# Last down products over 512 and 256 columns, squares of the last norm summed on VectorE, final scaling in two-row steps

## Chip, core and metric

One core of a Trainium2 chip runs the whole program. The metric is the device time of one execution in microseconds. The engines are TensorE (PE: matrix products, with PEld for the loading of weights), VectorE (DVE), ScalarE (ACT), GpSimd (POOL), and SyncE (SP), which here only issues DMAs.

## What is computed

A decoder layer for 2048 prompt tokens and 64 sample tokens of width 1024: a mixer (windowed attention and pooling), cross-attention into 256 memory tokens, a squared-ReLU MLP with 4096 hidden units, and a last RMS norm. Only the end matters here:

```python
h = _rmsnorm(x, g_ffn)
x = x + jnp.square(jax.nn.relu(h @ w_up)) @ w_down
...
y = _rmsnorm(x, g_final)     # x * rsqrt(mean(x*x) + 1e-5) * g_final
```

The inputs and outputs are float32. Each product is made of three products of rounded parts (`fp32r`): weight high by data high, weight high by data low, weight low by data high (`mm3`, lines 109 to 114).

## The kernel before

**Tiling.** Activations lie transposed: 128 of the 1024 features of a row of `x` on the partitions, tokens along the free axis. A token block has eight such rows, `bl.x(0)` to `bl.x(7)`, one behind the other in one tile, each `bl.n` columns wide. The tokens are worked through in three superblocks of two blocks (`SBLOCKS`, line 24): 384 and 384 columns, 256 and 320 (64 of them sample tokens), 384 and 384. In each superblock the whole layer runs, and at its end the MLP: 16 chunks of hidden units, each with an `up` (line 1283) and, for one chunk or for two at a time, a `down` (line 1331). `up` writes the squared-ReLU activations as high and low parts, 384 columns for each of the two halves of the columns, into `H`; in the first and last superblock half 0 is block 0 and half 1 is block 1 (`halves`, line 1175).

**The last down.** `down([NP - 2, NP - 1], ..., True, ...)` (line 1407) is the last one of a superblock, called with `fin`. It goes through half 0 first and then half 1 (`seq`, line 1333), eight rows `m` in each. For each row TensorE makes 12 products (four blocks of hidden units by three parts) into one PSUM bank `ps` out of four (`MM`); VectorE adds the bank onto `x` (line 1350, called the evacuation here); then `norm.sq(m)` takes the row's squares for the last norm.

**The last norm.** `Norm.sq` (line 234) has two ways. By default ScalarE squares the row (line 246 for the first, 249 for the others) and VectorE adds the squares up into `acc` (line 250); `fin` then sums `acc` over the partitions with one float32 product with a matrix of 1/1024 (line 258), which appears in the trace as two instructions. With `on_pe`, which is set for block 1 of the last superblock alone (line 1337), ScalarE squares each row (line 239) and TensorE adds it up in PSUM with a product of its own (line 242), eight pairs of instructions in all. `fin` ends with Ln and Exp on ScalarE (lines 261, 262) and three dependent steps on VectorE (lines 263 to 265), which give the factor `r` for each token.

**The final scaling.** `final(bl)` (line 1367) calls `fin`, multiplies the eight rows by `r` and the gain on VectorE (line 1371), and after each second row issues a store of two rows to `y` on SP (line 1373). It is put on a list `later` with a count (`DEFF`, line 370: 2), which `flush()` lowers; in the last down `flush` is called after the second and the fourth row of each four (line 1354). A `yield` in `final` would let the rest wait for the next `flush`; it is taken in the middle superblock only (`has`, line 1374). What is left on the list at the end is run by `flush(True)` (line 1416).

**Order.** The program is written in this order, but a planner puts each engine's instructions in their order before the kernel runs, and may pass one that is not ready. Within an engine the order then is fixed.

Of the kernel before, what the change touches and what calls it, by code (L numbers as in the profile page):

```python
# [11 lines left out]
AF = mybir.ActivationFunctionType  # L12
ALU = mybir.AluOpType

P = 128
NB = 384
SEQ = 2048
# [12 lines left out]
V_GMIX, V_GMEM, V_GCROSS, V_GFFN, V_GFINAL = 0, 8, 16, 24, 32  # L30
# [21 lines left out]
def kernel(ctx: ExitStack, tc: tile.TileContext, io, nW=12, nF=6, nT=10):  # L52
    nc = tc.nc
# [10 lines left out]
    TS = Slots([sb(f"t{i}", 400) for i in range(nT)])  # L64
    XT = [sb("x0", 3136), sb("x1", 3136)]
    MM = Slots([psp.tile([P, 512], F32, name=f"mm{i}", tag=f"mm{i}") for i in range(4)])
    AUX = Slots([psp.tile([P, 512], F32, name=f"aux{i}", tag=f"aux{i}") for i in range(4)])
# [6 lines left out]
    ones = sb("ones", P)  # L74
# [3 lines left out]
    vec = sb("vec", V_N)  # L78
# [27 lines left out]
    def w8(t):  # L106
        return t[:].rearrange("p (k c) -> p k c", c=P)

    def mm3(ps, ks, Wh, Wl, Hh, Hl, first=True, final=True):
        last = len(ks) - 1  # L110
        for i, k in enumerate(ks):
            nc.tensor.matmul(ps, Wh(k), Hh(k), start=first and i == 0, stop=False)  # L112
            nc.tensor.matmul(ps, Wh(k), Hl(k), start=False, stop=False)  # L113
            nc.tensor.matmul(ps, Wl(k), Hh(k), start=False, stop=final and i == last)  # L114
# [54 lines left out]
    NP = 16  # L169
# [38 lines left out]
    for s in range(3):  # L208
# [12 lines left out]
        for p in range(NP):  # L221
            add_up(s, p)
            pl = (p - 1, p) if p == NP - 1 or s == 1 and p % 2 else () if p == NP - 2 or s == 1 else (p,)
# [4 lines left out]
    class Norm:  # L228
        def __init__(self, n, x, on_pe=False, add=None):
            self.n, self.x, self.on_pe, self.add = n, x, on_pe, add or nc.vector  # L230
            self.acc = None
            self.pm = AUX.get() if on_pe else None

        def sq(self, k, eng=None):
            n = self.n
            if self.on_pe:
                t = TS.get()
                if eng is None:
                    nc.scalar.activation(t[:, 0:n], self.x(k), AF.Square)
                else:  # L240
                    eng.tensor_tensor(t[:, 0:n], self.x(k), self.x(k), ALU.mult)
                nc.tensor.matmul(self.pm[:, 0:n], ones[:], t[:, 0:n], start=k == 0, stop=k == 7)
                TS.put(t)
            elif self.acc is None:
                self.acc = TS.get()
                nc.scalar.activation(self.acc[:, 0:n], self.x(k), AF.Square)
            else:
                t = TS.get()
                nc.scalar.activation(t[:, 0:n], self.x(k), AF.Square)
                self.add.tensor_tensor(self.acc[:, 0:n], self.acc[:, 0:n], t[:, 0:n], ALU.add)  # L250
                TS.put(t)

        def fin(self):
            n = self.n
# [113 lines left out]
    later = []  # L368
    RW = 5
    DEF, DEFF = (1, 1), (2, 2)  # L370
# [188 lines left out]
    def superblock(s, blks, nxt):  # L559
        last, has = s == 2, s == 1  # L560
# [352 lines left out]
        while len(qdone) < len(lead):  # L913
            m = len(qdone)
# [257 lines left out]
        if has:  # L1172
            halves = [[(blks[0], 0, 0, 256), (blks[1], 288, 256, 32)], [(blks[1], 0, 0, 288)]]
        else:
            halves = [[(bl, 0, 0, bl.n)] for bl in blks]
        hn = halves[1][0][3]
        PT = 288 if has else NB
# [3 lines left out]
        tt = {}  # L1181
# [92 lines left out]
        def relu2(H, h, k, t):  # L1274
            for bl, c0, o, w in halves[h]:
                nc.vector.scalar_tensor_tensor(t[:, o:o + w], t[:, o:o + w], 0.0, bl.r3[:, c0:c0 + w], ALU.max, ALU.mult)
            nc.scalar.activation(t[:, 0:hn], t[:, 0:hn], AF.Square)
            hi, lo = H[4 * h + 2 * k], H[4 * h + 2 * k + 1]
            nc.scalar.copy(hi, t[:, 0:hn])  # L1279
            nc.vector.tensor_tensor(lo, t[:, 0:hn], f32(hi), ALU.subtract)  # L1280
            TS.put(t)

        def up(p, H=None):

            def prod(w, o, nm):
                ps = AUX.get()
                wk = [(lambda x: lambda i: x[0][:, x[1] + P * i:x[1] + P * i + P])(x) for x in zip(w, o)]
                mm3(ps[:, 0:hn], range(4), *wk, T(nm, 0), T(nm, 1))
                return ps

            def add(t, ps, r, free=True):
                nc.vector.tensor_tensor(t[:, 0:hn], ps[:, 0:hn], r[:, 0:hn], ALU.add)  # L1292
                if free:
                    AUX.put(ps)
                return t

            wa = S.next(("up", s, p, 0))
            p1 = prod(wa, (0, 0), "B11")
            r1 = TS.get()
            nc.scalar.copy(r1[:, 0:hn], p1[:, 0:hn])  # L1300
            AUX.put(p1)
            if H is None:
                H = own([tt.pop(("B11", 0)), tt.pop(("B11", 1))])
            if p == 0:
                flush()
            wb = S.next(("up", s, p, 1))
            p5 = prod(wb, (0, 0), "T1")
            flush()
            p6 = prod(wb, (512, 512), "T2")
            WS.put(*wb)  # L1310
            r2 = add(TS.get(), p6, r1)
            r4 = add(TS.get(), p5, r2, False)
            w22, *wd = S.next(("up", s, p, 2))
            add(r4, prod(wd, (512, 512), "B22"), r4)
            relu2(H, 1, 0, r4)
            flush()
            p7 = prod(wd, (0, 0), "T3")
            WS.put(*wd)
            add(r2, p7, r2)
            relu2(H, 1, 1, add(TS.get(), p5, r2))  # L1320
            p2 = prod(wa, (512, 512), "B21")
            WS.put(*wa)
            relu2(H, 0, 0, add(r1, p2, r1))
            flush()
            p4 = prod((w22, w22), (0, 512), "T4")
            WS.put(w22)
            relu2(H, 0, 1, add(r2, p4, r2))
            S.pump()
            return H

        def down(pl, Hs, fin=False, hook=None):
            K = range(2 * len(pl))
            seq = [(t, h) for h in (0, 1) for t in (0, 1)] if fin else [(t, h) for t in (0, 1) for h in (1, 0)]
            loaded, left, steps = {}, {}, 0
            if fin:
                for bl in blks:
                    bl.norm = Norm(bl.n, bl.x, on_pe=last and bl.b == 1)
            for t, h in seq:
                if t not in loaded:
                    loaded[t] = [S.next(("dn", s, p, t)) for p in pl]  # L1340
                    left[t] = 2
                w = loaded[t]
                for m4 in range(4):
                    m = 4 * t + m4
                    ps = MM.get()
                    mm3(ps[:, 0:hn], K, lambda k: w8(w[k // 2][0])[:, 2 * m4 + k % 2, :], lambda k: w8(w[k // 2][1])[:, 2 * m4 + k % 2, :],
                        lambda k: Hs[k // 2][4 * h + 2 * (k % 2)], lambda k: Hs[k // 2][4 * h + 2 * (k % 2) + 1])
                    for bl, c0, o, n in halves[h]:
                        x = bl.x(m, c0, c0 + n)
                        nc.vector.tensor_tensor(x, ps[:, o:o + n], x, ALU.add)  # L1350
                    if fin:
                        blks[h].norm.sq(m)
                    MM.put(ps)
                    if m4 == 3 or fin and m4 == 1:
                        steps += 1
                        if hook is not None:
                            hook(steps)
                        flush()
                left[t] -= 1
                if left[t] == 0:  # L1360
                    for x in w:
                        WS.put(*x)
                S.pump()
                if fin and t == 1:
                    later.append([DEFF[h], lambda h=h: final(blks[h])])

        def final(bl):
            bl.norm.fin()
            n = bl.n
            for k in range(8):  # L1370
                nc.vector.scalar_tensor_tensor(bl.x(k), bl.x(k), vec[:, V_GFINAL + k:V_GFINAL + k + 1], bl.norm.r[:, 0:n], ALU.mult, ALU.mult)  # L1371
                if k % 2 == 1:
                    nc.sync.dma_start(io["y"][:, bl.xo + (k - 1) * n:bl.xo + (k + 1) * n], XT[bl.b][:, (k - 1) * n:(k + 1) * n])
                    if has and k < 7:
                        yield
            TS.put(bl.norm.r)

        S.resF = 0
        Ht = [ACTS.get(), ACTS.get()]
        H = own(Ht)  # L1380
# [14 lines left out]
            rest0 = norm1_sums(nxt[0])  # L1395
        Hl = list(tt.values())
        H2 = up(NP - 1)
        for bl in blks:
            TS.put(bl.r3)
        ACTS.put(*tt.values())  # L1400
        Hl = [t for t in Hl if id(t) not in {id(x) for x in tt.values()}]
        hook = None
        if nxt is not None:
            S.resW = 4
            later.append([1, rest0])
            hook = lambda i: norm1(nxt[1], 1) if i == 5 else None
        down([NP - 2, NP - 1], [H, H2], True, hook)
        ACTS.put(*Ht, *Hl)

    TS2 = [sb(f"cp{i}", 512) for i in range(2)]  # L1410
# [139 lines left out]
```

## Time and profile before

| | |
|---|---|
| time, median of 3 runs | 2540.4 us (2538.5 to 2542.72) |
| the profiled execution's own time | 2537.34 us |
| its span, first to last instruction | 2535.3 us |
| TensorE busy in the span | 2483.3 us, 98% |
| VectorE busy | 1858.8 us, 73% |
| ScalarE busy | 1098.6 us, 43% |
| GpSimd busy | 172.5 us, 7% |
| granted TensorE clock, mean | 0.992 |

In the profile a line such as `L1371 DVE SCALAR_TENSOR_TENSOR x<-x,vec,t 128x384 f32` names the kernel's line, the engine, the operation, what is written from what, and the shape; buffer numbers are left out, so `x` is any part of the two `x` tiles and `t` any of ten scratch tiles. A busy TensorE is not one at its peak: its products are pipelined, so that one of 0.33 us starts each 0.17 us.

### The profile page before, as it was taken

What the parts mean: (1) busy time and instruction counts of PE and PEld (TensorE: products, weight loads), DVE (VectorE), ACT (ScalarE), POOL (GpSimd) and SP (SyncE); (2) the same over time, 40 slices, a digit from 0 to 9 for tenths busy, and PEclk for the clock granted to TensorE, in tenths of its full rate; (3) what the DMA queues carried; (4) which work ended last, traced back from release to release, by engine and by line L of the source; (5) the groups of instructions that cost most, each with busy time, mean ns of one, the idle gap of its engine ahead of it and who ended that gap; (6) DMA issues with size and microseconds to landing.
All of it is one profiled execution on the core that took longest, in us unless ns stands there. A gap on an engine that the chain in (4) does not pass through costs nothing.

```text
span 2535.3 us, 38897 instructions
## 1 busy us (share of the span) xinstructions
PE 2483.3 (98%) x15199; PEld 2368.2 (93%) x15199; DVE 1858.8 (73%) x3687; ACT 1098.6 (43%) x2131; POOL 172.5 (7%) x282
## 2 busy tenths in 40 slices
PE   9899999999999999999999999999999999999998
PEld 9798989999999998996899999989998999999997
DVE  8568537877777788863787877898745877777775
ACT  7666334433333344752544334457534433333332
POOL 0015010000000001411000000003301000000000
PEclk9999999999999999999999999999999999999999
DMA  8833211222222125246522222240412121222211
GB/s 289 270 122 104 92 34 59 67 67 67 67 67 67 61 81 154 82 148 237 212 92 100 76 92 92 88 143 26 142 42 68 42 67 67 67 67 68 67 58 50
DMA packets 92540, 244.73 MB, mean 97 GB/s; under 512 B 16772, under 2 KB 31556, under 8 KB 91204
## 3 DMA queue, kind: packets, MB, share of 16 engines
q1 hardware_dynamic: 92356, 242.25, 28.8%
q8 instruction: 119, 1.95, 0.3%
q14 instruction: 65, 0.53, 0.1%
HBM read 219.53 MB, written 22.69 MB: 96 GB/s over the span
## 4 chain that ended last, share of the span: by engine, by line
PE 78%; DVE 4%; ACT 1%; DMA 1%; POOL 1%; issue 0%; POOLq 0%; DVEq 0%; ACTq 0%
PE mm L112 11%; PE mm L113 11%; PE mm L114 11%; PE aux L112 9%; PE aux L113 9%; PE aux L114 9%; PE mm L352 5%; PE mm L354 5%; PE mm L353 5%; PE aux L754 1%; PE aux L785 1%; DVE x L1371 1%; PE aux L1082 0%; ACT w L118 0%; DVE t L300 0%
## 5 line engine op out<-in xcount | busy, mean ns | idle before, releaser
L118 ACT CAST w<-f 128x1024 fp32r<-128x1024 f32 x378 | 395.6, 1050 | 731.5 <-PE mm L114 366.6
L119 DVE TENSOR_TENSOR w<-f,w 128x1024 fp32r<-128x1024 f32 x378 | 460.4, 1222 | 185.6 <-PE aux L113 98.3
L113 PE MATMUL mm<-act,w 128*128 128x384 f32 (+2 forms) x1728 | 552.8, 320 | 0.0
L114 PE MATMUL mm<-act,w 128*128 128x384 f32 (+2 forms) x1728 | 550.7, 319 | 0.8 <-DVE w L119 0.8
L112 PE MATMUL mm<-act,w 128*128 128x384 f32 (+2 forms) x1728 | 537.9, 321 | 3.4 <-DVE t L459 2.2
L112 PE MATMUL aux<-act,w 128*128 128x384 f32 (+1 forms) x1344 | 432.4, 322 | 3.6 <-DVE t L264 2.7
L114 PE MATMUL aux<-act,w 128*128 128x384 f32 (+1 forms) x1344 | 432.1, 322 | 0.0
L113 PE MATMUL aux<-act,w 128*128 128x384 f32 (+1 forms) x1344 | 431.9, 321 | 0.0
L352 PE MATMUL mm<-act,w 128*128 128x384 f32 (+2 forms) x1248 | 408.7, 328 | 7.3 <-DVE x L1350 2.9
L354 PE MATMUL mm<-act,w 128*128 128x384 f32 (+2 forms) x1248 | 405.1, 325 | 3.2 <-DVE w L119 3.1
L353 PE MATMUL mm<-act,w 128*128 128x384 f32 (+2 forms) x1248 | 405.9, 325 | 1.6 <-DVE act L302 1.2
L1350 DVE TENSOR_TENSOR x<-mm,x 128x384 f32<-128x384 f32 (+3 forms) x672 | 313.8, 493 | 125.8 <-PE mm L114 124.1
L112 PEld LDWEIGHTS mm<-act,w 128*128 128x128 f32 x1728 | 322.8, 189 | 13.3 <-ACT act L1279 7.0
L113 PEld LDWEIGHTS mm<-act,w 128*128 128x128 f32 x1728 | 326.5, 189 | 5.4 <-DVE act L1280 3.8
L114 PEld LDWEIGHTS mm<-act,w 128*128 128x128 f32 x1728 | 326.1, 189 | 2.0 <-DVE w L119 1.0
L112 PEld LDWEIGHTS aux<-act,w 128*128 128x128 f32 x1344 | 252.7, 188 | 4.8 <-DVE t L264 3.2
L114 PEld LDWEIGHTS aux<-act,w 128*128 128x128 f32 x1344 | 253.4, 189 | 0.3
L113 PEld LDWEIGHTS aux<-act,w 128*128 128x128 f32 x1344 | 253.5, 189 | 0.0
L352 PEld LDWEIGHTS mm<-act,w 128*128 128x128 f32 x1248 | 238.8, 191 | 13.7 <-issue 3.9
L353 PEld LDWEIGHTS mm<-act,w 128*128 128x128 f32 x1248 | 238.7, 191 | 7.4 <-DVE act L302 2.8
L354 PEld LDWEIGHTS mm<-act,w 128*128 128x128 f32 x1248 | 238.5, 191 | 5.6 <-DVE w L119 4.9
L1292 DVE TENSOR_TENSOR t<-aux,t 128x384 f32<-128x384 f32 (+1 forms) x336 | 169.4, 517 | 24.4 <-PE aux L114 18.7
(227 smaller groups left out, 3001.2 us busy)
## 6 DMA issues: line engine op xcount, KB each, us to landing
f<-in_wup SPq DMA_DIRECT2D x96, 512.0 KB, 3.7
f<-in_wdn SPq DMA_DIRECT2D x96, 512.0 KB, 3.7
f<-in_win SPq DMA_DIRECT2D x30, 512.0 KB, 3.8
f<-a_s SPq DMA_DIRECT2D x24, 512.0 KB, 3.8
f<-b_s SPq DMA_DIRECT2D x24, 512.0 KB, 4.4
x<-in_x SPq DMA_DIRECT2D x6, 1536.0 KB, 7.4
f<-in_wco SPq DMA_DIRECT2D x16, 512.0 KB, 5.3
f<-in_cmk SPq DMA_DIRECT2D x16, 512.0 KB, 4.4
```

The costliest lines, as they stand in the source:

```text
L112: nc.tensor.matmul(ps, Wh(k), Hh(k), start=first and i == 0, stop=False)
L113: nc.tensor.matmul(ps, Wh(k), Hl(k), start=False, stop=False)
L114: nc.tensor.matmul(ps, Wl(k), Hh(k), start=False, stop=final and i == last)
L118: nc.scalar.copy(th[:], r[:, 0:1024])
L119: nc.vector.tensor_tensor(tl[:], r[:, 0:1024], f32(th[:]), ALU.subtract)
L352: nc.tensor.matmul(ps[:, 0:n], w8(th)[:, k, :], hi(b, k), start=k == 0, stop=False)
L353: nc.tensor.matmul(ps[:, 0:n], w8(th)[:, k, :], lo(b, k), start=False, stop=False)
L354: nc.tensor.matmul(ps[:, 0:n], w8(tl)[:, k, :], hi(b, k), start=False, stop=k == 7)
L754: nc.tensor.matmul(o, q[:, j, c0:c0 + P], kz[kv][hl][:, so + k0:so + 256], start=hl == 0, stop=hl == 1)
L785: nc.tensor.transpose(ps[:, P * j:P * j + P], u.Lv[:, j, P * kb:P * kb + P], ident[:])
L1292: nc.vector.tensor_tensor(t[:, 0:hn], ps[:, 0:hn], r[:, 0:hn], ALU.add)
L1350: nc.vector.tensor_tensor(x, ps[:, o:o + n], x, ALU.add)
```

## The change

- In the last superblock the last `down` no longer works on 384 and 384 columns but on 512 (all of block 0 and the first 128 columns of block 1) and 256 (the rest of block 1). A group of 512 has two evacuations, of 384 and of 128 columns.
- The last norm of that superblock is kept for three column parts: block 0 (384), the first 128 columns of block 1, and its last 256. The first two sum their squares on VectorE, as block 0 did. The third, in place of eight pairs of products, adds rows 0 to 6 on VectorE into `acc`, brings `acc` into PSUM with one pair, and adds row 7 with another.
- `final` runs for each part. Its pieces of two rows are now parted by `yield` in the last superblock as well; `flush` is called after every row of the last `down`; the first part becomes due at the next flush, the second at the one after.
- The stores of the two parts of block 1 take two rows of 128 or of 256 columns out of rows 384 wide; the host puts `y` together from these pieces.
- For the sake of the 512 columns the high and low activations lie in another order in `H`, in all superblocks: the index is `4*k + 2*hl + h` in place of `4*h + 2*k + hl` (k: block of hidden units, hl: high or low, h: half), so that both halves of one part lie side by side.

```diff
-        def sq(self, k, eng=None):
+        def sq(self, k):
             n = self.n
-            if self.on_pe:
+            if self.on_pe and k == 7:
                 t = TS.get()
-                if eng is None:
-                    nc.scalar.activation(t[:, 0:n], self.x(k), AF.Square)
-                else:
-                    eng.tensor_tensor(t[:, 0:n], self.x(k), self.x(k), ALU.mult)
-                nc.tensor.matmul(self.pm[:, 0:n], ones[:], t[:, 0:n], start=k == 0, stop=k == 7)
+                nc.scalar.activation(t[:, 0:n], self.x(k), AF.Square)
+                nc.tensor.matmul(self.pm[:, 0:n], ones[:], t[:, 0:n], start=False, stop=True)
                 TS.put(t)
...
                 self.add.tensor_tensor(self.acc[:, 0:n], self.acc[:, 0:n], t[:, 0:n], ALU.add)
                 TS.put(t)
+                if self.on_pe and k == 6:
+                    self.pm = AUX.get()
+                    nc.tensor.matmul(self.pm[:, 0:n], ones[:], self.acc[:, 0:n], start=True, stop=False)
+                    TS.put(self.acc)
...
-            hi, lo = H[4 * h + 2 * k], H[4 * h + 2 * k + 1]
+            hi, lo = H[4 * k + h], H[4 * k + 2 + h]
...
+        if last:
+            ends = []
+            b0, b1 = blks
+            for c0, n, pieces, parts in (
+                    (0, 512, [(b0, 0, 0, 384), (b1, 0, 384, 128)], [part(b0, 0, 384), part(b1, 0, 128)]),
+                    (512, 256, [(b1, 128, 0, 256)], [part(b1, 128, 256)])):
+                ends.append((n, (lambda c0, n: lambda W, k, hl: W[2 * k + hl][:, c0:c0 + n])(c0, n), pieces, parts))
...
-                    mm3(ps[:, 0:hn], K, lambda k: w8(w[k // 2][0])[:, 2 * m4 + k % 2, :], lambda k: w8(w[k // 2][1])[:, 2 * m4 + k % 2, :],
-                        lambda k: Hs[k // 2][4 * h + 2 * (k % 2)], lambda k: Hs[k // 2][4 * h + 2 * (k % 2) + 1])
-                    for bl, c0, o, n in halves[h]:
-                        x = bl.x(m, c0, c0 + n)
-                        nc.vector.tensor_tensor(x, ps[:, o:o + n], x, ALU.add)
+                    mm3(ps[:, 0:n], K, lambda k: w8(w[k // 2][0])[:, 2 * m4 + k % 2, :], lambda k: w8(w[k // 2][1])[:, 2 * m4 + k % 2, :],
+                        lambda k: mv(Hs[k // 2], k % 2, 0), lambda k: mv(Hs[k // 2], k % 2, 1))
+                    for bl, c0, o, wd in pieces:
+                        x = bl.x(m, c0, c0 + wd)
+                        nc.vector.tensor_tensor(x, ps[:, o:o + wd], x, ALU.add)
                     if fin:
-                        blks[h].norm.sq(m)
+                        for p in parts:
+                            p.norm.sq(m)
                     MM.put(ps)
-                    if m4 == 3 or fin and m4 == 1:
+                    if m4 == 3 or fin and (m4 == 1 or last):
...
-                    later.append([DEFF[h], lambda h=h: final(blks[h])])
+                    for i, p in enumerate(parts):
+                        later.append([(1 if last else DEFF[h]) + i, lambda p=p: final(p)])
...
-                    nc.sync.dma_start(io["y"][:, bl.xo + (k - 1) * n:bl.xo + (k + 1) * n], XT[bl.b][:, (k - 1) * n:(k + 1) * n])
-                    if has and k < 7:
+                    nc.sync.dma_start(io["y"][:, yo + (k - 1) * n:yo + (k + 1) * n].rearrange("p (k n) -> p k n", n=n), bl.xv[:, k - 1:k + 1, p.c0:p.c0 + n])
+                    if s > 0 and k < 7:
                         yield
...
+        if last:
+
+            H, H2 = [[t[:, PT * i:PT * i + 2 * PT] for t in ts for i in (0, 2)] for ts in (Ht, [x for x in Hl if id(x) not in {id(y) for y in tt.values()}])]
+            cols = ends
```

More of the change, by code (lines that the diff above doesn't have):

```diff
@@ L231, in __init__ @@
             self.acc = None
-            self.pm = AUX.get() if on_pe else None
-        def sq(self, k, eng=None):
+            self.pm = None
+        def sq(self, k):
             n = self.n
-            if self.on_pe:
+            if self.on_pe and k == 7:
                 t = TS.get()
-                if eng is None:
-                    nc.scalar.activation(t[:, 0:n], self.x(k), AF.Square)
-                else:
-                    eng.tensor_tensor(t[:, 0:n], self.x(k), self.x(k), ALU.mult)
-                nc.tensor.matmul(self.pm[:, 0:n], ones[:], t[:, 0:n], start=k == 0, stop=k == 7)
+                nc.scalar.activation(t[:, 0:n], self.x(k), AF.Square)
+                nc.tensor.matmul(self.pm[:, 0:n], ones[:], t[:, 0:n], start=False, stop=True)
                 TS.put(t)
@@ L1329, in up, with part, down @@
             return H
-        def down(pl, Hs, fin=False, hook=None):
+        def part(bl, c0, n):
+            p = FB()
+            p.bl, p.c0, p.n = bl, c0, n
+            p.x = lambda k: bl.x(k, c0, c0 + n)
+            return p
+        cols = []
+        for h in range(2):
+            cols.append((hn, (lambda h: lambda H, k, hl: H[4 * k + 2 * hl + h])(h), halves[h], [part(blks[h], 0, blks[h].n)]))
+        if last:
[5 more added lines that the diff above has]
+                ends.append((n, (lambda c0, n: lambda W, k, hl: W[2 * k + hl][:, c0:c0 + n])(c0, n), pieces, parts))
+        def down(pl, Hs, fin=False, hook=None, cols=cols):
             K = range(2 * len(pl))
@@ L1335, in down @@
             if fin:
-                for bl in blks:
-                    bl.norm = Norm(bl.n, bl.x, on_pe=last and bl.b == 1)
+                for h in range(2):
+                    for p in cols[h][3]:
+                        p.norm = Norm(p.n, p.x, on_pe=last and h == 1)
             for t, h in seq:
@@ L1342, in down @@
                 w = loaded[t]
+                n, mv, pieces, parts = cols[h]
                 for m4 in range(4):
@@ L1364, in down, with final @@
                 if fin and t == 1:
-                    later.append([DEFF[h], lambda h=h: final(blks[h])])
-        def final(bl):
-            bl.norm.fin()
-            n = bl.n
+                    for i, p in enumerate(parts):
+                        later.append([(1 if last else DEFF[h]) + i, lambda p=p: final(p)])
+        def final(p):
+            p.norm.fin()
+            n, yo, bl = p.n, p.bl.xo + 8 * p.c0, p.bl
             for k in range(8):
-                nc.vector.scalar_tensor_tensor(bl.x(k), bl.x(k), vec[:, V_GFINAL + k:V_GFINAL + k + 1], bl.norm.r[:, 0:n], ALU.mult, ALU.mult)
+                nc.vector.scalar_tensor_tensor(p.x(k), p.x(k), vec[:, V_GFINAL + k:V_GFINAL + k + 1], p.norm.r[:, 0:n], ALU.mult, ALU.mult)
                 if k % 2 == 1:
-                    nc.sync.dma_start(io["y"][:, bl.xo + (k - 1) * n:bl.xo + (k + 1) * n], XT[bl.b][:, (k - 1) * n:(k + 1) * n])
-                    if has and k < 7:
+                    nc.sync.dma_start(io["y"][:, yo + (k - 1) * n:yo + (k + 1) * n].rearrange("p (k n) -> p k n", n=n), bl.xv[:, k - 1:k + 1, p.c0:p.c0 + n])
+                    if s > 0 and k < 7:
                         yield
-            TS.put(bl.norm.r)
+            TS.put(p.norm.r)
         S.resF = 0
@@ L1406, in superblock @@
             hook = lambda i: norm1(nxt[1], 1) if i == 5 else None
-        down([NP - 2, NP - 1], [H, H2], True, hook)
+        down([NP - 2, NP - 1], [H, H2], True, hook, cols)
         ACTS.put(*Ht, *Hl)
@@ L1532 @@
             n = npr + ns
-            yb = o["y"][:, 8 * xo:8 * (xo + n)].reshape(P, 8, n).transpose(2, 1, 0).reshape(n, 1024)
-            xo += n
+            ws = (128, 256) if t0 + npr == SEQ else (n,)
+            yb = []
+            for w in ws:
+                yb.append(o["y"][:, 8 * xo:8 * (xo + w)].reshape(P, 8, w).transpose(2, 1, 0).reshape(w, 1024))
+                xo += w
+            yb = np.concatenate(yb, 0)
             yp.append(yb[:npr])
```

## The prediction

> **What bounds the kernel now.** First the page: its span is what the sum is made against. Then the busy time by stretch, cut where the last down's half 0, half 1 and the tail end.
>
> ```profile
> span 2535.3 us, 38897 instructions
> ```
>
> ```profile
> core 0: us, PE busy (x) PEld busy (x) DVE busy (x) ACT busy (x) POOL busy (x), PEclk, DMA share, GB/s
> 2483.17:2500.25 17.08, 17.08 (x98) 16.67 (x98) 9.93 (x19) 6.09 (x13) 0.00 (x0) 1.00 0.00 0
> 2500.25:2521.34 21.09, 21.09 (x109) 18.38 (x107) 10.18 (x19) 4.25 (x8) 0.00 (x0) 1.00 0.12 48
> 2521.34:2535.30 13.96, 2.20 (x6) 1.05 (x6) 7.08 (x14) 2.56 (x5) 0.00 (x0) 0.75 0.38 155
> ```
>
> TensorE is busy through both halves; VectorE is busy 10.18 of half 1's 21.09 us. Behind the last product lies a tail of 13.96 us in which TensorE works 2.20. So only some 52 us of the 2535 are touched, and two things can shorten: TensorE's time, and the tail. The profiled execution took 2537.34 us, 2.0 more than its span; the median of the runs shown, 2540.4, is 3.1 above that.
>
> Now the order of time, VectorE and then ScalarE:
>
> ```profile
> 2516.70 4.32 DVE L1371 SCALAR_TENSOR_TENSOR x<-x,vec,t 128x384 f32<-128x384 f32 x8
> 2520.95 1.48 DVE L1350 TENSOR_TENSOR x<-mm,x 128x384 f32<-128x384 f32 x3
> 2525.51 0.56 DVE L263 SCALAR_TENSOR_TENSOR t<-t 128x384 f32<-128x384 f32 x1 [3.09 <-ACT t L262]
> 2526.11 0.56 DVE L264 SCALAR_TENSOR_TENSOR t<-aux,t 128x384 f32<-128x384 f32 x1
> 2526.70 0.56 DVE L265 SCALAR_TENSOR_TENSOR t<-t,t 128x384 f32<-128x384 f32 x1
> 2527.29 4.32 DVE L1371 SCALAR_TENSOR_TENSOR x<-x,vec,t 128x384 f32<-128x384 f32 x8
> ```
>
> ```profile
> 2521.53 1.45 ACT L239 ACTIVATE t<-x 128x384 f32<-128x384 f32 x3 [6.02 <-DVE x L1350]
> 2524.34 0.58 ACT L261 ACTIVATE t<-aux,eps 128x384 f32<-128x384 f32 x1 [1.36 <-PE aux L242]
> 2524.96 0.52 ACT L262 ACTIVATE t<-t 128x384 f32<-128x384 f32 x1
> ```
>
> Block 0's eight scalings hold VectorE from 2516.70, in one run, and three evacuations queue behind them until 2520.95. The last evacuation ends at 2522.43; call that point E. From E the chain is squares, their products, Ln, Exp, three steps, eight scalings to 2531.61, and 3.69 us of store: 12.87 in all.
>
> **The change, part by part.** *TensorE's products.* Rows with the spacing of 256 and of 512 columns:
>
> ```profile
> 20.04 0.28 PE L112 MATMUL mm<-act,w 128*128 128x256 f32 x1
> ...
> 21.84 0.28 PE L112 MATMUL mm<-act,w 128*128 128x256 f32 x1
> ```
>
> ```profile
> 84.22 0.40 PE L112 MATMUL mm<-w,act 128*128 128x512 f32 x1
> ...
> 86.04 0.39 PE L114 MATMUL mm<-w,act 128*128 128x512 f32 x1
> ```
>
> Fifteen products of 256 in 1.80 us are 0.120 each, eight of 512 in 1.82 are 0.2275. For 384, half 0 gives 17.08/98 = 0.174. So 0.3475 stands against 0.348 for a pair of each: the new split costs TensorE nothing by itself. The weight loads stay hidden at 256 columns, as these rows show. The Trainium skill ("TensorE: Matmul & The Clock Gate", Back-to-back issue gap) gives N/2.4 + 2.5 ns for one product alone and warns that this is too little at small N, because each weight load takes part in the spacing. At 256 columns the formula gives 109 ns where the trace shows 120, so it would be off by about 1 us over 96 products; the sum keeps the trace's spacing.
>
> *TensorE's squares and sums*, from the chain of waits:
>
> ```profile
> 2503.72 0.73 PE aux L242 x2
> ...
> 2513.01 0.65 PE aux L258 x2
> ...
> 2522.11 2.22 PE aux L242 x6
> ```
>
> ```profile
> L258 PE MATMUL aux<-t,ones 128*128 128x256 f32 x8 | 2.5, 391 | 0.0
> ```
>
> Before, five pairs of L242 (0.73 or somewhat more) and one L258 stand inside half 1, about 4.4 us, and three pairs behind it. Afterwards half 1 holds one pair of 384 (0.65), one of 128 (no row; between 0 and the 0.63 of 256, 2.5/4, I take 0.35, near a third to a half of the widths shown), and of the part's two pairs of 256 at most one.
>
> *VectorE.* Durations by shape:
>
> ```profile
> L250 DVE TENSOR_TENSOR t<-t,t 128x256 f32<-128x256 f32 x35 | 14.7, 419 | 1.5 <-ACT t L249 0.9
> ...
> L1371 DVE SCALAR_TENSOR_TENSOR x<-x,vec,t 128x384 f32<-128x384 f32 x32 | 17.4, 611 | 0.1
> ...
> L1371 DVE SCALAR_TENSOR_TENSOR x<-x,vec,t 128x256 f32<-128x256 f32 x8 | 3.6, 474 | 0.0
> ```
>
> In a run they start closer than they last: eight scalings of 0.611 take 4.32, 0.53 each; three evacuations of 0.56 take 1.48, 0.46 each. I carry these overlaps (0.08 and 0.10) to other widths. Extrapolated linearly, 128 columns last 0.34 (scaling) and 0.28 (evacuation, add).
>
> Let T be the end of half 0. Half 0 starts its products at 2483.17 as before; 96 by 0.2275 are 21.84, and the 0.4 us that the 17.08 hold beyond 96 by 0.1735 I keep. T = 2505.4.
>
> *By TensorE*, half 1 then takes 8 by 12 by 0.120 = 11.5, and 0.65 + 0.35 + 0.63: T + 13.2, and with the last evacuation E = T + 13.6.
>
> *By VectorE*, between T and E now lie: (a) row 7 of half 0, two evacuations and two adds, 2 by 0.46 and 2 by 0.18 = 1.3; (b) block 0's three steps at 0.59 and eight scalings at 0.53 = 6.0; (c) the 128-column part's three steps at 0.31 and eight scalings at 0.26 = 3.0; (d) eight evacuations and six new adds of 256 columns, between 0.32 and 0.42 each, mostly with a wait ahead, so 0.35 = 4.9. That is 15.2. VectorE also waits early on: block 0's factor is ready only after its last add (T + 1.9), the pair (0.65), Ln (0.58), Exp (0.52) and hand-overs, T + 3.85, while two evacuations of 0.4 are all there is to do: 1.05 idle, with further hand-overs 1.5 (bounds 0 and 2.5). E = T + 16.7 = 2522.1, against 2522.43 before.
>
> So VectorE, not TensorE, sets E: the 3 us that TensorE saves are hidden by the six adds and by the second part's eleven instructions. The two-row steps do not help here either, since all pieces are written ahead of row 5's evacuation: they spread the same work. Stalls of TensorE behind a full set of four PSUM banks cost nothing more for the same reason.
>
> *The tail* with 256 columns:
>
> ```profile
> L249 ACT ACTIVATE t<-x 128x256 f32<-128x256 f32 x28 | 11.0, 405 | 6.6 <-DVE x L1233 4.0 <-DVE x L1350 2.6
> ...
> L261 ACT ACTIVATE t<-aux,eps 128x256 f32<-128x256 f32 x4 | 1.9, 471 | 0.4 <-PE aux L258 0.4
> ...
> L262 ACT ACTIVATE t<-t 128x256 f32<-128x256 f32 x4 | 1.7, 414 | 0.0
> ```
>
> Square 0.45 with its hand-over; one or both pairs, 0.7 to 1.4, I take 1.0; Ln and Exp 0.97; three steps at 0.45 = 1.38; eight scalings, seven by 0.40 and 0.47 = 3.27; then the store.
>
> ```profile
> out_y<-x SPq DMA_DIRECT2D x16, 384.0 KB, 2.3
> ...
> out_y<-x SPq DMA_DIRECT2D x4, 256.0 KB, 2.4
> ```
>
> A smaller store lands no sooner, so the 3.69 stay (bounds 0.3 either way for rows of 1 KB taken out of longer ones). Twelve stores are issued in place of eight, 0.33 us each on a queue with nothing else to do. Sum 10.76, against 12.87: 2.1 less.
>
> **Sum.** 0.3 from E and 2.1 from the tail: span 2535.3 - 2.4 = 2532.9, execution 2534.9, and on the median 2540.4 - 2.4 = 2538.0. E between T + 15.2 and T + 17.7, and the second pair, give 2535.9 to 2539.4 for this case.
>
> The Trainium skill ("VectorE: DVE Perf Modes", The DRAIN you can't avoid) says that the next operation does not start until the pipeline has emptied, which speaks against more and narrower VectorE instructions. The trace differs: eight scalings of 0.611 would take 4.89, and took 4.32. The third rival below is what it would give.
>
> The new order of `H` moves addresses, not instructions. It would cost if the waits were kept for whole tiles, since a half's parts now share tiles with the other half's. The run at 2516.70 excludes that: its rows went on at 0.53 while stores of earlier rows of the same tile were being read.
>
> **The rivals.**
> 1. *TensorE sets E.* If the planner leaves 3 us of scalings of the first two parts behind the last evacuation, they fill VectorE's idle time there (square, pairs, Ln, Exp: 2.4 us; 3.09 idle before). E = T + 13.6 = 2519.0, the tail as above: 5.5 less, 2534.9. For it: that gap is real. Against: these pieces stand earlier in the program, and at 2516.70 the planner let scalings go ahead of evacuations.
> 2. *Slower: a store holds an evacuation.* The stores of the 128-column part take rows k-1 and k out of 384; from the first to the last address that stretch includes the other 256 columns of row k-1. If the planner keeps whole stretches apart, the evacuations of rows 4 and 6 must wait for the stores of rows 4, 5 and 6, 7, and all VectorE work queues behind them. One such wait is at most a landing, 2.3, with the hand-over near 2.7. It decides from 2.4 us on: two waits of 1.4 to 2.7 give 2540.8 to 2543.4. Against: part of each passes under queued work. The trace of before has only whole rows and cannot exclude it.
> 3. *Each VectorE instruction costs its full duration*, because most wait for a hand-over: (a) 1.7, (b) 6.7, (c) 3.7, (d) 5.9, in all 18.0 and not 15.2: 2540.8, no gain at all. The part of the change that shortens the tail is then paid in full by half 1.
>
> **How the numbers follow.** The forecast has 0.66, rival 1 0.14, rival 2 0.10, rival 3 0.10. A run here differs from the next by about 2 us either way (2538.5 to 2542.72), and 0.2%, 5.1 us, is about what a measurement can tell from no change. Only the better half of rival 1 lies below 2535.3, and only an outlying rival 2 above 2545.5: faster 0.10, same 0.86, slower 0.04. The range takes in rival 1's 2534.9 and most of rival 2: 2534.5 to 2542.5.
>
> **What would show it.** Right: products 0.228 and 0.120 apart; VectorE nearly without idle time from T + 4 to E; E near 2522; TensorE idle at times in half 1; eight 256-column scalings of 3.3 us at the end; span near 2533. Wrong: scalings of 384 columns behind the last evacuation (rival 1), an evacuation released by a DMA (rival 2), runs of scalings no denser than their durations (rival 3), or a spacing at 512 or 256 columns other than shown.

## The result, and the profile after

| | before | changed |
|---|---|---|
| median | 2540.4 us (13 runs, 2533.26 to 2543.61) | 2534.97 us (13 runs, 2531.69 to 2538.04) |
| ratio, 95% interval | | 0.998 (0.9971 to 0.9989) |
| profiled execution, its span | 2537.34, 2535.3 us | 2537.09, 2535.2 us |

The change is faster by 0.2%, 5.4 us by the medians; the whole interval lies below 1. The two profiled executions, however, have the same span. Two executions of one kernel differ by several microseconds: in two traces of the changed kernel the last low-part write of `up` starts at 2487.46 and at 2484.74. So the traces have to be compared over stretches between events that both have. Two such stretches carry the case. The **end stretch** runs from the last low-part write of `up` (line 1280 before, 1281 after) to the last instruction; the **middle stretch** from the first to the last evacuation of 288 columns in the middle superblock.

End stretch, from the timeline of VectorE in the changed kernel (start, duration, engine, line). Line 1371 is now the evacuation, 247 the add of squares, 264 to 266 the three steps of `fin`, 1394 the scaling:

```profile
2487.46 0.56 DVE L1281 TENSOR_TENSOR act<-t,act 128x384 fp32r<-128x384 f32 x1 [0.20 <-ACT act L1280]
...
2507.22 0.76 DVE L1371 TENSOR_TENSOR x<-mm,x 128x384 f32<-128x384 f32 x2 [0.75 <-PE mm L114]
...
2511.28 0.55 DVE L264 SCALAR_TENSOR_TENSOR t<-t 128x384 f32<-128x384 f32 x1
...
2514.81 1.67 DVE L1394 SCALAR_TENSOR_TENSOR x<-x,vec,t 128x384 f32<-128x384 f32 x4
2516.39 0.41 DVE L1371 TENSOR_TENSOR x<-mm,x 128x256 f32<-128x256 f32 x1
2516.73 0.60 DVE L1394 SCALAR_TENSOR_TENSOR x<-x,vec,t 128x128 f32<-128x128 f32 x2
...
2521.89 0.43 DVE L247 TENSOR_TENSOR t<-t,t 128x256 f32<-128x256 f32 x1
2522.24 1.08 DVE L1371 TENSOR_TENSOR x<-mm,x 128x256 f32<-128x256 f32 x3
2523.23 0.95 DVE L247 TENSOR_TENSOR t<-t,t 128x256 f32<-128x256 f32 x2
2527.30 0.43 DVE L264 SCALAR_TENSOR_TENSOR t<-t 128x256 f32<-128x256 f32 x1 [3.12 <-ACT t L263]
2527.76 0.42 DVE L265 SCALAR_TENSOR_TENSOR t<-aux,t 128x256 f32<-128x256 f32 x1
2528.22 0.42 DVE L266 SCALAR_TENSOR_TENSOR t<-t,t 128x256 f32<-128x256 f32 x1
2528.68 3.26 DVE L1394 SCALAR_TENSOR_TENSOR x<-x,vec,t 128x256 f32<-128x256 f32 x8
```

Row 7 of half 0 is there at T = 2507.2, the last evacuation ends at E = 2523.3. From the first step of `fin` on, VectorE goes without a gap to 2524.2. The end stretch is 2535.2 - 2487.46 = 47.7 us; before it was 2535.3 - 2485.65 = 49.65. That is 1.9 us of the 5.4.

The busy time by stretch of the changed kernel, half 0, half 1, tail:

```profile
2485.00:2507.19 22.19, 22.19 (x99) 17.94 (x98) 12.51 (x32) 7.47 (x20) 0.00 (x0) 1.00 0.00 0
2507.19:2522.30 15.11, 13.06 (x100) 12.04 (x99) 13.17 (x36) 4.35 (x11) 0.00 (x0) 1.00 0.32 116
2522.30:2535.20 12.90, 2.07 (x4) 1.17 (x4) 6.31 (x17) 2.00 (x5) 0.00 (x0) 0.53 0.32 111
```

In half 1 TensorE (first column after the length) is no longer always busy, 13.06 of 15.11 us. In the tail stands a granted clock of 0.53; a cut around the last two pairs of products, lines 251 and 239, tells more. TensorE's rows of these pairs follow it:

```profile
2520.50:2524.20 3.70, 0.36 (x4) 0.15 (x2) 3.57 (x11) 1.53 (x4) 0.00 (x0) 0.84 0.53 186
2524.20:2526.40 2.20, 2.07 (x4) 1.17 (x4) 0.00 (x0) 0.06 (x1) 0.00 (x0) 0.50 0.00 0
```

```profile
2524.23 1.22 PE L251 MATMUL aux<-t,ones 128*128 128x256 f32 x2 [3.38 <-DVE t L247]
2525.25 1.06 PE L239 MATMUL aux<-t,ones 128*128 128x256 f32 x2
```

TensorE had been idle for 3.4 us, and both pairs ran at half clock, 2.07 us.

Middle stretch: first and last evacuation of 288 columns, before, and then changed:

```profile
1308.99 0.45 DVE L1350 TENSOR_TENSOR x<-mm,x 128x288 f32<-128x288 f32 x1
...
1669.35 0.45 DVE L1350 TENSOR_TENSOR x<-mm,x 128x288 f32<-128x288 f32 x1
```

```profile
1312.89 0.45 DVE L1371 TENSOR_TENSOR x<-mm,x 128x288 f32<-128x288 f32 x1
...
1671.04 0.45 DVE L1371 TENSOR_TENSOR x<-mm,x 128x288 f32<-128x288 f32 x1
```

360.36 us became 358.15, although the change touches nothing there but the order of `H`. TensorE's timeline shows where: twelve products make a row, and before one of them stood out as slow. The same four products of the same row, before and then changed:

```profile
1360.56 0.30 PE L112 MATMUL mm<-act,w 128*128 128x288 f32 x1
1360.69 0.31 PE L113 MATMUL mm<-act,w 128*128 128x288 f32 x1
1360.84 0.30 PE L114 MATMUL mm<-act,w 128*128 128x288 f32 x1
1360.98 0.29 PE L112 MATMUL mm<-act,w 128*128 128x288 f32 x1
```

```profile
1363.98 0.30 PE L112 MATMUL mm<-act,w 128*128 128x288 f32 x1
1364.12 0.29 PE L113 MATMUL mm<-act,w 128*128 128x288 f32 x1
1364.25 0.29 PE L114 MATMUL mm<-act,w 128*128 128x288 f32 x1
1364.37 0.29 PE L112 MATMUL mm<-act,w 128*128 128x288 f32 x1
```

Before, the last product of the row ahead of this one started at 1360.03 (its evacuation began at 1360.36), so 1360.69 is the fifth of the next row: high weights by the low part of the second block, line 113. The next starts 0.15 us behind it, where its neighbours keep 0.13 to 0.14 (changed, from 1364.12, it is 0.13), and the same comes back at 1362.31. From the recorded starts of the first seven of the eight pairs of chunks (112 rows), 89 of 448 products of line 113 take more than 143 ns to the next start before, and 9 of 448 after.

These slow products are only the part that a limit of 143 ns catches. By position in the row, the median distance from the fifth product to the next start was 145 ns and became 133. The second product (high weights by the low part of the first block) and the sixth went from 139 to 131 each. The twelve mean distances, without waits (distances of 250 ns or more), add up to 1613 ns before and 1594 after: 0.019 us for each of 112 rows, 2.1 us of the 2.2.

### The profile page after: what moved, and what is told of

Its sections match the earlier page's. It is cut to its first block, busy times and chain, and to the rows that moved or that the text cites. A ratio compares the mean times of both kernels' runs of the same rounds, so it can differ in the third digit from the quotient of the medians.

```text
span 2535.2 us, 38934 instructions
## 1 busy us (share of the span) xinstructions
PE 2482.2 (98%) x15189; PEld 2363.5 (93%) x15189; DVE 1864.4 (74%) x3719; ACT 1099.8 (43%) x2141; POOL 173.5 (7%) x282
## 4 chain that ended last, share of the span: by engine, by line
PE 77%; DVE 5%; ACT 1%; DMA 1%; POOL 1%; issue 0%; POOLq 0%; DVEq 0%; ACTq 0%; SPq 0%
PE mm L112 11%; PE mm L113 11%; PE mm L114 11%; PE aux L112 9%; PE aux L113 9%; PE aux L114 9%; PE mm L355 5%; PE mm L353 5%; PE mm L354 5%; PE aux L755 1%; DVE x L1394 1%; PE aux L786 1%; DVE t L301 0%; DVE w L119 0%; DVE t L247 0%
## 5 line engine op out<-in xcount | busy, mean ns | idle before, releaser
L113 PE MATMUL mm<-act,w 128*128 128x384 f32 (+3 forms) x1728 | 551.5, 319 | 0.0
L114 PE MATMUL mm<-act,w 128*128 128x384 f32 (+3 forms) x1728 | 548.5, 318 | 1.9 <-DVE w L119 1.9
L112 PE MATMUL mm<-act,w 128*128 128x384 f32 (+3 forms) x1728 | 537.9, 321 | 3.4 <-DVE t L460 2.2
L353 PE MATMUL mm<-act,w 128*128 128x384 f32 (+2 forms) x1248 | 408.2, 327 | 7.3 <-DVE x L1371 2.9
L355 PE MATMUL mm<-act,w 128*128 128x384 f32 (+2 forms) x1248 | 405.0, 325 | 2.7 <-DVE w L119 2.6
L354 PE MATMUL mm<-act,w 128*128 128x384 f32 (+2 forms) x1248 | 405.5, 325 | 1.6 <-DVE act L303 1.2
L1371 DVE TENSOR_TENSOR x<-mm,x 128x384 f32<-128x384 f32 (+4 forms) x680 | 315.0, 491 | 118.8 <-PE mm L114 116.6
```

What stands on the lines that cost most here:

```text
L353: nc.tensor.matmul(ps[:, 0:n], w8(th)[:, k, :], hi(b, k), start=k == 0, stop=False)
L354: nc.tensor.matmul(ps[:, 0:n], w8(th)[:, k, :], lo(b, k), start=False, stop=False)
L355: nc.tensor.matmul(ps[:, 0:n], w8(tl)[:, k, :], hi(b, k), start=False, stop=k == 7)
L1371: nc.vector.tensor_tensor(x, ps[:, o:o + wd], x, ALU.add)
```

## The experiments

The stretches of every kernel that was run, in microseconds. The two kernels of the comparison, the new order of `H` alone, the changed kernel with the old order and the last kernel ran nine times or more; each of the seven others ran once, so only its stretches are read and not its time.

| kernel | middle | end | slow products of line 113 |
|---|---|---|---|
| before | 360.4 | 49.6 | 89 of 448 |
| changed; run again | 358.2; 358.2 | 47.7; 47.9 | 9; 5 |
| before with new order of `H` | 358.2 | 49.6 | 6 |
| changed with old order of `H` | 360.6 | 47.8 | 96 |
| before, `H` 384 columns apart | 357.6 | 49.6 | 12 |
| before, `H` moved by 256 columns | 360.8 | 49.6 | 103 |
| changed, all squares on TensorE | 358.2 | 46.1 | 7 |
| changed, no two-row steps | 358.2 | 46.9 | 11 |
| changed, idle products in the tail | 358.1 | 46.8 | 9 |
| changed, adds on GpSimd | 358.2 | 47.9 | 7 |
| changed, late squares on TensorE | 358.2 | 45.1 | 10 |
| the same, `H` 384 columns apart | 357.7 | 45.1 | 12 |

The stretches repeat to 0.2 us in most cases (0.5 in the middle between those with the old order), while whole executions spread over several. So small effects are read from them.

**1. The two parts of the gain.** The new order of `H` alone in the kernel before:

```diff
-            hi, lo = H[4 * h + 2 * k], H[4 * h + 2 * k + 1]
+            hi, lo = H[4 * k + h], H[4 * k + 2 + h]
...
-                        lambda k: Hs[k // 2][4 * h + 2 * (k % 2)], lambda k: Hs[k // 2][4 * h + 2 * (k % 2) + 1])
+                        lambda k: Hs[k // 2][4 * (k % 2) + h], lambda k: Hs[k // 2][4 * (k % 2) + 2 + h])
```

> The kernel before with the new order of H alone, in all superblocks. Theory A (the order of H in the middle superblock costs TensorE some 0.02 us in each row of a down, by one slow low-part product of 0.145 us among twelve; the changed kernel shed it): in the middle superblock the distance over five pairs of chunks falls by 1.7 to 1.8 us as between the two traces, products of line 113 above 143 ns fall from 87 of 383 to under 20, and the time falls by 2 to 3 us, ratio 0.9988 to 0.9992. The end (from the last low-part write of up to the last instruction) stays 49.6 us. Rival B (the middle superblock differs by chance between two executions, and the order of H is worth nothing): the slow products stay, ratio 1.000.

The middle stretch went from 360.4 to 358.2. Over five pairs of chunks (from the first evacuation of 288 columns in the second pair to the first in the seventh) 240.56 us became 238.72, 1.84 less, about as expected. The slow products are gone, and the end is unchanged: theory A. By time this cannot be seen: 2540.33 us, ratio 0.9996 (0.9987 to 1.0005).

The rest of the change without it:

```diff
-            hi, lo = H[4 * k + h], H[4 * k + 2 + h]
+            hi, lo = (H[4 * k + h], H[4 * k + 2 + h]) if last else (H[4 * h + 2 * k], H[4 * h + 2 * k + 1])
...
-... lambda H, k, hl: H[4 * k + 2 * hl + h])(h), halves[h] ...
+... lambda H, k, hl: H[4 * k + 2 * hl + h] if last else H[4 * h + 2 * k + hl])(h), halves[h] ...
```

> The changed kernel, with the old order of H kept in the first two superblocks. Theory A: the slow products of line 113 are back (80 to 95 of some 383), the end stays at 47.7 us against 49.65 before, so only some 1.9 us of the change is left: ratio about 0.9992. Rival B: no slow products, and the ratio that of the change, 0.998.

Slow products back, end 47.8; ratio 0.9995 (0.9985 to 1.0005). Theory A in the trace. The change itself once more:

> The changed kernel once more, on the same chip as the two others. Theory A: ratio 0.998 to 0.9985 (1.9 us at the end and 2.3 in the middle superblock, in all 4.2), that is the sum of the two parts. Rival B: the whole of 5.4 us comes from the end or from chance: the ratio is that of the run with the old order of H.

2534.53 us, ratio 0.9979 (0.997 to 0.9988). By the traces the parts are 2.4 us (360.6 to 358.2, means of the runs with each order at 288 columns) and 1.8 us, 4.2 in all, 0.17%, inside this interval. The medians of the three runs alone do not add up as well (0.04% and 0.05% against 0.21%); their intervals are wide enough for it, but whether the whole holds another microsecond beyond the two stretches is not settled.

**2. What makes the product slow.** Two kernels that only move `H` in the middle superblock, old order kept. In the first its pieces lie 384 columns apart and not 288:

```diff
-        H = own(Ht)
+        H = [t[:, NB * i:NB * i + hn] for t in Ht for i in range(4)]
```

> The kernel before with the old order of H, but in the middle superblock the eight pieces of H lie 384 columns apart and not 288 (the second set, in the tiles of the sums, is left). Where the slow product is that of the second block's low part (fourth piece of the tile, bytes 3456 to 4608): if its place in the tile matters (the fourth piece straddling byte 4096, or lying right behind the high part), it is gone, under 20 of some 383 above 143 ns. If the order in which tiles alternate matters and not the place, 80 to 95 stay.

12 of 448: gone, and the stretch is 0.5 us shorter still than with the new order. In the second they stay 288 apart but begin at column 256:

```diff
-        H = own(Ht)
+        o = 256 if has else 0
+        H = [t[:, o + PT * i:o + PT * i + hn] for t in Ht for i in range(4)]
```

> The kernel before with the old order of H, whose pieces in the middle superblock stay 288 columns apart but begin at column 256 of the tile and not at 0. The slow product was the one that reads the fourth piece, bytes 3456 to 4608 of the tile. If crossing byte 4096 makes it slow, it is now the third piece (3328 to 4480), read by lines 112 and 114: those are slow and line 113 is not (under 20 of some 383 above 143 ns). If following the high part of the second block makes it slow, line 113 keeps 80 to 95. If neither, all three lines run at 0.132.

Line 113 keeps its slow products, 103 of 448; lines 112 and 114 have 7 and 0, as they had before and have after the change. So crossing byte 4096 is not the reason. What the kernels with slow products have in common is that in `H` the low part of a block follows its high part at 288 columns (1152 bytes); with 1536 bytes (the first trial) or 2304 (the new order) it is gone. The first block's low part, which follows at the same distance, is slower too, only below the limit of 143 ns (139 ns against 131, above). Byte 3456 as the start of the low part does not do it alone either: in the new order the second half's low part begins there, and only 9 of 448 products are slow.

But the distance alone is not the cause. The products of `up` in the same superblock read their inputs at the same 1152 bytes (`T`, lines 1187 to 1190), and there, in the kernel before, the fifth of twelve has a median of 131 ns. A place of the pair that repeats every 1024 bytes, which the second trial does not change, is not excluded. So it is shown that the layout of `H` makes the products slow, and which distances do not; the mechanism is open.

**3. What the end still pays.** All squares of the last part on TensorE again, as before:

```diff
-            if self.on_pe and k == 7:
+            if self.on_pe:
+                if k == 0:
+                    self.pm = AUX.get()
...
-                nc.tensor.matmul(self.pm[:, 0:n], ones[:], t[:, 0:n], start=False, stop=True)
+                nc.tensor.matmul(self.pm[:, 0:n], ones[:], t[:, 0:n], start=k == 0, stop=k == 7)
```

> The changed kernel, but the last part of 256 columns takes all its squares on TensorE again (eight pairs of products, no adds on VectorE). The end is counted from the last low-part write of up to the last instruction: 49.65 us before, 47.8 us changed. Theory A (VectorE sets E in the changed kernel, and its adds and the slow pairs at half clock cost what TensorE saves): VectorE sheds 2.1 us of adds, TensorE takes 7 pairs of about 0.55 into half 1 and sets E near T + 17.0, and the tail loses the last adds and one slow pair, some 1.9 us; end 46.3 to 47.3. Rival B (moving the squares to VectorE is what brought the gain): TensorE's 3 us come back, end 49 to 51.

End 46.1: 1.7 us *shorter* than the changed kernel, a little below theory A's range. Rival B falls: the move of the squares to VectorE cost time. But E did not come sooner by the four adds that stand ahead of it in the changed kernel (some 0.34 us each, 1.4 in all), and TensorE did not set it at T + 17 as theory A had it. This kernel's VectorE:

```profile
2509.31 0.42 DVE L1373 TENSOR_TENSOR x<-mm,x 128x256 f32<-128x256 f32 x1 [0.56 <-PE mm L114]
2511.86 0.89 DVE L266 SCALAR_TENSOR_TENSOR t<-t 128x384 f32<-128x384 f32 x2 [2.13 <-ACT t L265]
...
2521.33 1.07 DVE L1373 TENSOR_TENSOR x<-mm,x 128x256 f32<-128x256 f32 x3
2524.80 0.43 DVE L266 SCALAR_TENSOR_TENSOR t<-t 128x256 f32<-128x256 f32 x1 [2.39 <-ACT t L265]
```

T is 2506.4 here, so the first step of `fin` starts at T + 5.4 and not T + 4.1: on TensorE the pair of row 0 (at 2509.31) went ahead of block 0's own sum, which began at 2509.84 = T + 3.4 and not T + 1.8, and VectorE waited for the factor. From there on VectorE has no gap until E. E = 2522.4 = T + 16.0, as good as unchanged; 1.5 us of the gain lie behind E, where no adds and no slow pairs are left.

The two-row steps taken out of the last superblock:

```diff
-                    if s > 0 and k < 7:
+                    if has and k < 7:
```

> The changed kernel, but the scaling of the last superblock is not parted into steps of two rows: eight rows in one go for each part. Theory A (the steps only spread the same VectorE work): end 47.4 to 48.2. Rival B (the steps let evacuations through and spare TensorE a wait that sets the end): TensorE stands still for 3 us or more in half 1 behind full banks and the end grows to 49 or more.

End 46.9, 0.8 us better than with the steps, outside both expectations. E is at T + 16.2 as it was, so the steps did only spread the work. The gain stands behind E: in one run the scalings held TensorE up earlier behind full banks, its last row came later, its idle time before the last pairs was 1.4 us, and they took 1.1 us, not 2.1, at a granted clock of 1.00:

```profile
2522.76 0.70 PE L251 MATMUL aux<-t,ones 128*128 128x256 f32 x2 [1.38 <-DVE t L247]
2523.30 0.59 PE L239 MATMUL aux<-t,ones 128*128 128x256 f32 x2
```

That points to the clock. The direct trial adds 24 products of no use behind the last row's:

```diff
+                    if last and fin and h == 1 and m == 7:
+                        keep = AUX.get()
+                        for i in range(24):
+                            nc.tensor.matmul(keep[:, 0:n], w8(w[i % 2][0])[:, i % 8, :], mv(Hs[i % 2], i // 2 % 2, 0), start=i == 0, stop=i == 23)
+                        AUX.put(keep)
```

> The changed kernel with 24 idle products of 256 columns into a spare bank behind the last row's products (2.9 us), whose result is not used. Theory A (after 3.4 us without work TensorE is granted half its clock, and the last two pairs take 2.1 us in place of 1.1): granted clock 1.0 at the pairs, which take 1.0 to 1.3 us together, end 46.7 to 47.0. Rival B (the pairs are slow for another reason, or the idle products come to lie on the path): pairs still 2 us, or begin later; end 47.8 or more.

The planner let 8 of them run between earlier rows; 16 stand in the gap behind the last row, 2.08 us, and leave 1.46 us of idle time ahead of the pairs. The pairs, in the busy time by stretch:

```profile
2521.10:2522.40 1.30, 1.13 (x4) 0.68 (x4) 0.06 (x1) 0.02 (x1) 0.00 (x0) 1.00 0.00 0
```

Clock 1.00, 1.13 us in place of 2.07, end 46.8, and E at T + 16.1 as it was: theory A. Then the six adds on GpSimd:

```diff
-                        p.norm = Norm(p.n, p.x, on_pe=last and h == 1)
+                        p.norm = Norm(p.n, p.x, on_pe=last and h == 1, add=nc.gpsimd if last and h == 1 else None)
```

> The changed kernel, with the last part's six adds of squares on GpSimd and not on VectorE. Theory A (VectorE sets E): it sheds 2.1 us, GpSimd takes 0.6 to 0.9 us for each add of 256 columns beside it; E near T + 14.2, but the last add, of row 6, ends some 0.5 us later behind E; end 46.0 to 47.0. Rival B (E is not set by VectorE's work but by the order of the parts): end 47.5 to 48.5. Rival C (GpSimd and VectorE slow one another): VectorE's scalings and evacuations become longer by a tenth or more, end 48 or more.

End 47.9, no gain; E came to T + 15.5 only. Theory A's range is missed, and the number is rival B's, but E did move. VectorE and GpSimd held one another up:

```profile
2517.14 1.66 DVE L1394 SCALAR_TENSOR_TENSOR x<-x,vec,t 128x128 f32<-128x128 f32 x4
2518.72 0.41 DVE L1371 TENSOR_TENSOR x<-mm,x 128x256 f32<-128x256 f32 x1
2519.05 2.35 DVE L1394 SCALAR_TENSOR_TENSOR x<-x,vec,t 128x128 f32<-128x128 f32 x4
```

```profile
2517.81 1.57 POOL L247 TENSOR_TENSOR t<-t,t 128x256 f32<-128x256 f32 x1 [4.59 <-ACT t L246]
2519.72 0.74 POOL L247 TENSOR_TENSOR t<-t,t 128x256 f32<-128x256 f32 x1 [0.34 <-ACT t L246]
2522.33 2.38 POOL L247 TENSOR_TENSOR t<-t,t 128x256 f32<-128x256 f32 x3 [1.87 <-ACT t L246]
```

Each of the two rows of line 1394 holds two scalings of 128 columns and two of 384, though it names one shape only. In the first the scalings kept their length and the GpSimd add beside them took 1.57 us in place of 0.74 (spans on GpSimd are rough). In the second the add that began at 2519.72 took 0.74, and the scaling of 384 columns beside it 1.16 us in place of 0.60. Three VectorE instructions beside GpSimd adds were longer, by 0.95 us together, so of the 1.4 us of adds that VectorE shed ahead of E little was left. GpSimd's last add ended 1.5 us behind E (VectorE's had ended 0.9 behind it), and TensorE, idle for 3.9 us, ran both pairs at half clock again, 2.1 us. This part of rival C is borne out, though its end of 48 or more is just missed.

**4. A version with a shorter end than both.** Rows 0 and 1 on VectorE, whose one add falls where it is idle for the factor anyway; rows 2 to 7 on TensorE, which keeps working:

```diff
-            if self.on_pe and k == 7:
+            if self.on_pe and k > 1:
...
-                nc.tensor.matmul(self.pm[:, 0:n], ones[:], t[:, 0:n], start=False, stop=True)
+                nc.tensor.matmul(self.pm[:, 0:n], ones[:], t[:, 0:n], start=False, stop=k == 7)
...
-                if self.on_pe and k == 6:
+                if self.on_pe and k == 1:
```

> The first alteration of the last kernel alone: rows 0 and 1 on VectorE, rows 2 to 7 on TensorE. Theory A: end 45.0 to 45.8, the middle superblock as in the changed kernel (266.1 us over the stretch that took 268.3 before). Rival: end 46.1 or more.

With `H` 384 columns apart added, as in the first trial under 2:

> The changed kernel with two alterations: the last part takes rows 0 and 1 on VectorE and rows 2 to 7 on TensorE (so that VectorE's one add falls into its early idle time and TensorE keeps working), and H in the middle superblock lies 384 columns apart. Theory A (VectorE's adds, a late factor and the half clock are what the changed kernel still pays): E near T + 15, pairs at full clock, end 45.0 to 45.8 against 47.8 changed and 49.6 before; the middle superblock 0.5 us shorter over five pairs of chunks; ratio to the kernel before 0.9965 to 0.9977. Rival (E stays at T + 16 whatever is taken off VectorE, because TensorE's pairs push the rest back): end 46.1 or more, as with all squares on TensorE.

End 45.1 in both, middle stretch 358.2 and 357.7, as theory A had it. (What stretch the expectation's 266.1 us are is not said there; over the five pairs of chunks used above the first of these kernels takes 238.71 us and the changed one 238.76.) One add stands ahead of E here and four in the changed kernel: at 0.34 us each that is 1.0 us less, and E came at T + 15.05 and not T + 16.1. That fits VectorE setting E. The second kernel took 2531.87 us (9 runs), ratio to the kernel before 0.9969 (0.9959 to 0.9979). This interval overlaps that of the changed kernel (0.9971 to 0.9989), so that it is the faster of the two is read from the stretches, 3.1 us together, and not from the times alone. Its halves 0 and 1 and tail:

```profile
2481.00:2504.60 23.60, 23.60 (x108) 19.36 (x107) 13.94 (x35) 7.88 (x20) 0.00 (x0) 1.00 0.00 1
2504.60:2519.70 15.10, 14.94 (x109) 13.63 (x109) 13.12 (x35) 5.03 (x13) 0.00 (x0) 1.00 0.36 132
2519.70:2530.00 10.30, 1.38 (x6) 0.87 (x6) 4.53 (x11) 1.32 (x4) 0.00 (x0) 0.80 0.33 115
```

Half 1 now has TensorE busy for 14.94 of 15.10 us and VectorE for 13.12: neither waits long for the other. The three pairs behind the last evacuation took 1.56 us at a granted clock of 1.00 (the 0.80 is the mean of the whole tail).

## Why the prediction was right or wrong

The sign held, and who sets E was right, but the number was met in part by luck. The median, 2534.97, lies 0.5 us inside the range's lower end, which was drawn there for rival 1's 2534.9, and rival 1 did not happen. The interval that the prediction gave for its own case, 2535.9 to 2539.4, was missed, and the median stands on the side of 2535.3 to which it gave 0.10. Of the 2.4 us forecast the end stretch shows 1.9, with two errors that partly cancel (E 0.6 us sooner against the forecast, the tail 1.1 us longer). Another 2.2 us came from a term that the prediction put at nothing, and the rest of the 5.4 is not assigned to any stretch.

- *Products at 0.2275 and 0.120, T.* Right. T was forecast 19.75 us behind the last low-part write (2505.4 - 2485.65), and came 19.74 behind it.
- *VectorE sets E, TensorE's saving is hidden.* Right: forecast T + 16.7, measured T + 16.1, TensorE idle at times in half 1. Against the last low-part write E came 0.9 us sooner than before, forecast 0.3. The sum put all six adds of squares ahead of E; those of rows 5 and 6 came behind it, 0.9 us, so that E's gain is in part a loss of the tail. VectorE's idle time ahead of E was 1.9 us, a little more than the 1.5 taken.
- *The tail, 10.76.* Mis-sized: 11.9 from E. Steps, Ln, Exp and scalings came as worked out (3.26 for the scalings, 3.27 forecast), the store 3.3 and not 3.69. The term that was too small is "square 0.45, one or both pairs 1.0": it took 3.0, because the adds of rows 5 and 6 ended 0.9 us behind E, and both pairs stood behind them at half clock, 2.07 us. The forecast saw that TensorE would have gaps in half 1, but not what the last gap does to its clock.
- *"The new order of H moves addresses, not instructions", cost nothing.* Wrong: it was worth 2.2 to 2.4 us in the middle superblock, as much as all that was forecast. The row quoted for it excluded one mechanism, waits kept for whole tiles, and was taken for all of them; the prediction shows no row of the superblock with 288 columns, where a product in twelve already stood out.
- *The rivals.* TensorE did not set E. No evacuation of rows 4 or 6 was released by a DMA: those at 2520.99 and in the run at 2522.24 follow VectorE's own work without a gap, so the strided stores held nothing. Scalings ran denser than their durations (the four from 2514.81 on, two of 384 columns at 0.611 and two of 128 at 0.344, would have lasted 1.91 and took 1.67), so the third fell too. The section of the Trainium skill that the prediction sets against the trace here ("VectorE: DVE Perf Modes", The DRAIN you can't avoid) says as well that a next operation that is not held starts earlier, so trace and section need not differ.
- *The two-row steps.* "They spread the same work" held for E (T + 16.1 with them, T + 16.2 without), but by letting TensorE finish early they cost 0.8 us behind it, where the pairs took 2.07 us at half clock with them and 1.13 without.
- *"About 2 us either way" from run to run.* Too small: the 13 runs of the kernel before lie between 2533.26 and 2543.61.

## What to carry to other kernels

A change of layout "for the sake of" another edit is a change of its own: look at the spacing of the products that read it in every stage, not only in the stage that the edit is about. Where one engine's work is hidden behind another's, ask also what its idle time does to its own next instruction; here 3.4 us without a product nearly doubled the price of the last two pairs. When whole executions spread by more than the effect, compare stretches between the same two events in several traces: here they repeat to a few tenths of a microsecond, where the interval from 13 runs of each kernel is 4.6 us wide. When slow cases are counted against a limit, look also at what lies just below it: here it hid the second and the sixth product of each row.

## What the hardware showed unexpectedly

After 3.4 us without a product the granted clock was 0.50 at the next ones, and two pairs of float32 products of 256 columns took 2.07 us in place of 1.13. The Trainium skill ("TensorE: Matmul & The Clock Gate", What's actually happening) states that the array falls back to half its clock after an idle window of about 3.4 us; the trace agrees: 3.4 us (and 3.9 with the adds on GpSimd) were followed by half clock, and 1.4 and 1.5 us of idle time (no two-row steps, idle products) left it at full speed. What happens between 1.5 and 3.4 us these runs do not show.

In the products of `down` in the middle superblock, with 288 columns, the low part in `H` 1152 bytes behind the high part went with slower products: of the twelve of a row the fifth took 145 ns against 133 (medians), the second and the sixth 139 against 131. Twice that distance or 1536 bytes removed it; moving all pieces by 1024 bytes did not. The products of `up`, at the same distance, were not slow (131 ns). The cause is open.
